# A fourth weight buffer with loads issued one chunk earlier, a descriptor area of 8 KB, and a moved product in the attention

## The chip, the cores and the metric

The kernel runs on one core of a Trainium2 chip. The metric is device time in microseconds (us) of one execution, as a median over runs.

## The reference

One layer of a streaming encoder over 512 tokens of width 2048 (chunks of 64, fp32 inputs and outputs):

```
h = rms_norm(x);  proj = h @ w_in            # 2048 x 15424, cut into 13 parts
A: o_conv = (b * conv3(c * u) * silu(conv_z)) @ w_conv_out
B: q = rms_norm(c_q) @ w_uq (16 heads, 128 + 64 rotary);  k, v = rms_norm(c_kv) @ w_ukv
   softmax(block-causal(q k^T * scale)) v, times silu(mla_z), @ w_mla_out
C: cross-attention of mem_q (4 heads of 256) into 256 memory tokens
   k, v = rms_norm(mem) @ w_mem_kv;  times silu(mem_z), @ w_mem_out
x + (sigmoid(g_conv) * o_conv + sigmoid(g_mla) * o_mla + sigmoid(g_mem) * o_mem) @ w_o
```

## The kernel before, in words

Every product is made of three matmuls (`mm3`, L161 to L163): both sides are split into a rounded high part and a low rest, and high x high, high x low and low x high are summed in PSUM. A weight chunk of 512 KB is loaded from HBM into a tile `raw`, copied to its high part `whi` by ScalarE (ACT, L154 or L277), and VectorE (DVE) subtracts to get the low part `wlo` (L155 or L278). Three of the large products (`w_h`, `w_mla_out`, `w_o`) save matmuls with sums of quarter blocks: for those DVE also forms sums of the loaded weights first (L272 to L274). TensorE then runs 42 matmuls of 256 columns a chunk.

`raw` has three buffers, `whi` and `wlo` two each. The chunks stand in one list, `queue`. `take()` is called when TensorE's program comes to a chunk: it has the split of this chunk and the next one issued, and then `begin()` issues the load of the chunk after that together with its sums, as one step. A job is a generator that yields after its load (and sums), and then after its split.

The order of the work: the memory keys and values (32 chunks of `w_mem_kv`, during which the rows of x are read for the norm (`x_rows`), `x_scale` turns their scales by four transposes, and `x_pair` builds the input tiles); the panels of `w_h` (240 loads of 512 KB, to about 1340 us); the latent attention; the memory's attention with the convolution's output product; `w_mla_out`; `w_mem_out`; `w_o`.

Each engine runs its own queue in order. The order of TensorE (PE) and of the load queue SyncE (SP) is the order in which the program issues; so is DVE's in two stretches (from the end of the memory's product to the first panels, and from `w_mem_out` to the start of `w_o`). ACT, and DVE elsewhere, get their order from the compiler's planner, which models durations. A load waits on SP until the buffer it writes is free, and whatever SP was given later waits behind it.

In the attention one turn of the loop computes the keys' and values' projection of a pair of heads (`w`, 16 units), then the queries' one. Into these units an order written by hand slots the older pair: capital letters are its first (`A`) and second (`B`) head, small letters (`a`, `b`) the next pair's. A head's steps are transposes of keys and queries, four score steps, four transposes of the probabilities, and the product with the values, which also loads the gate tile `z` for the pair (L1004) and multiplies by it on DVE (L1010). In ORDER_KV of before, `A` alone is that last product of the first head, after the fourth `w`; the second head's product is the `B` in ORDER_Q after `a a a`.

Of the kernel before, what the change touches and what calls it, by code (L numbers as in the profile page):

```python
# [20 lines left out]
F32 = mybir.dt.float32  # L21
F32R = mybir.dt.float32r
I32 = mybir.dt.int32
AF = mybir.ActivationFunctionType
ALU = mybir.AluOpType
# [5 lines left out]
P = 128  # L31
# [17 lines left out]

ORDER_KV = "2w B B B w B w A 6w B w B B B 5w"
ORDER_Q = "a a a B a a a 4w a w b b 5w a 4w a w a a w"
ORDER_KV1 = "16w"
ORDER_Q1 = "6w a a w a 2w a a a w a w b b 3w a w a w a a"
# [52 lines left out]
def body(ctx, tc, a, out):  # L108
    nc = tc.nc
    act, vec, pool = nc.scalar, nc.vector, nc.gpsimd  # L110
# [7 lines left out]
    wpool = ctx.enter_context(tc.tile_pool(name="wts", bufs=2))  # L118
# [17 lines left out]

    def raw_tile():

        return wpool.tile([P, 8, 256], F32, tag="raw", name="raw", bufs=3)

    def weight_parts():
        return (wpool.tile([P, 7, 256], F32R, tag="whi", name="whi"),
# [2 lines left out]
    def flat(t):  # L145
        return t.rearrange("p s n -> p (s n)")
# [20 lines left out]
    queue = []  # L167
# [1 line left out]
    fills = []  # L169

    def upcoming(*jobs):
        queue.extend([job, None] for job in jobs)

    def begin(at):

        if at < len(queue) and queue[at][1] is None:
            queue[at][1] = queue[at][0]()
            queue[at].append(next(queue[at][1]))

    def take(ahead=1):  # L180
        for at, entry in enumerate(queue[:1 + ahead]):
            begin(at)
            if entry[2] is None:
                entry[2] = next(entry[1])
        begin(1 + ahead)
        if fills:
            fills.pop(0)()
        return queue.pop(0)[2]

    def plain_jobs(srcs, n, cut=False, parts=(), beside=None):  # L190

        held = []
        each = 2048 // (KC * n)

        def job(at):
            def go():
                if at % each == 0:
                    t = flat(raw_tile())  # L200
                    held.append(t)
                    for c in range(min(each, len(srcs) - at)):
                        step = n if cut and at + c == 0 else KC * n
                        for o in range(0, KC * n, step):
                            nc.sync.dma_start(t[:, c * KC * n + o:c * KC * n + o + step],
                                              srcs[at + c][:, o:o + step])
                        if beside is not None:
                            beside(at + c)
                yield
                o = at % each * KC * n  # L210
                yield weights(held[at // each][:, o:o + KC * n], n, cut and at == 0,
                              parts[at % len(parts)] if parts else None)
            return go
        return [job(at) for at in range(len(srcs))]
# [52 lines left out]
    def pair_weights(src):  # L267


        f = raw_tile()  # L270
        nc.sync.dma_start(flat(f[:, 0:4]), src)
        vec.tensor_tensor(out=f[:, 4:6], in0=f[:, 1:3], in1=f[:, 0:1].to_broadcast([P, 2, 256]), op=ALU.add)  # L272
        vec.tensor_tensor(out=f[:, 6], in0=f[:, 5], in1=f[:, 1], op=ALU.add)  # L273
        vec.tensor_tensor(out=f[:, 7], in0=f[:, 6], in1=f[:, 3], op=ALU.add)  # L274
        yield
        hi, lo = weight_parts()
        act.activation(hi, f[:, 1:8], AF.Copy)  # L277
        vec.tensor_tensor(out=lo, in0=f[:, 1:8], in1=r32(hi), op=ALU.subtract)  # L278
        yield hi, lo
# [150 lines left out]
    def memory_load(c):  # L430
        if c < 8:
            mraw[c] = pst.tile([P, KC, M], F32, tag="msq", name="mraw", bufs=5)
            nc.sync.dma_start(mraw[c], a["memT"][:, c * KC:(c + 1) * KC])
# [85 lines left out]
    def staged_parts():  # L519
# [1 line left out]

    memory_load(0)
    upcoming(*plain_jobs([a["w_mem_kv"][grp][c] for grp in range(4) for c in range(8)], 512, True,
                         (staged_parts, None, None), lambda c: memory_load(c + 1)))
    work = panels(xp, a["w_h"], len(SEQUENCE), lambda n: make(n), lambda n, e: finish(n, e), "aux")
    queue.insert(32 + 15, [lambda: rotary_weights(), None])
    parts_of_x = all_parts()
    manual_dve = ExitStack()
    for grp in range(4):
        banks = [bank("acc") for _ in range(2)]  # L530

        for n in dense_units(banks, 512, mT, "T", nk=KB, before=memory_chunk if grp == 0 else None,
# [5 lines left out]
                manual_dve.enter_context(tc.manual_schedule(engines={DVE}))  # L538
            if grp == 0:
                memory_squares(c)  # L540
            if c == 2:
                while later:
                    later.pop(0)("aux")
# [30 lines left out]
                nc.scalar.dma_start(mvdram[2 * (grp - 2) + i], t)  # L574
    for _ in parts_of_x:
        pass
    begin(2)
    close_st()
    close_mt()
    pxb, close_xb = open_pool("xb", "right")  # L580
# [7 lines left out]
    def rotary_weights():  # L588
        f = flat(raw_tile())
        nc.sync.dma_start(f[:, :1024], a["w_kr"])  # L590
        vec.tensor_tensor(out=f[:, 1024:1536], in0=f[:, 0:512], in1=f[:, 512:1024], op=ALU.add)
        yield
        hi, lo = (flat(t)[:, :1536] for t in weight_parts())
        act.activation(hi, f[:, :1536], AF.Copy)
        vec.tensor_tensor(out=lo, in0=f[:, :1536], in1=r32(hi), op=ALU.subtract)
        yield hi, lo
# [525 lines left out]
    def mem_attend(head):  # L1122
# [12 lines left out]
        for i2 in range(2):  # L1135
# [16 lines left out]
            ri = pq.tile([P, 2], F32, tag="ri", name="ri", bufs=2)  # L1152
            vec.reciprocal(ri, sm)
            for ii in range(2):
                vec.tensor_scalar(out=p[:, ii], in0=p[:, ii], scalar1=ri[:, ii:ii + 1], scalar2=None,
                                  op0=ALU.mult)
                pr.append(p[:, ii])
            yield
        pts = []
# [272 lines left out]

# [10 lines left out]
```

## Time and profile before

| | |
|---|---|
| median of 3 runs | 2172.43 us (2167.9 to 2177.55) |
| the profiled execution | 2174.51 us |
| its span, first to last instruction | 2172.7 us |
| granted TensorE clock, mean over the span | 0.995 |
| busy | PE 98%, PEld (weight load) 94%, DVE 80%, ACT 46%, POOL 6% |

1.8 us of the profiled execution lie outside its span. A busy share is a sum over stages that have different limits; the clock is a share of full speed (1.0 is the upper of its two levels, 0.5 the lower one), and PE's busy time includes time at the lower level.

### The profile page before, as it was taken

What the parts mean: (1) busy time and instruction counts of PE and PEld (TensorE: products, weight loads), DVE (VectorE), ACT (ScalarE), POOL (GpSimd) and SP (SyncE); (2) the same over time, 40 slices, a digit from 0 to 9 for tenths busy, and PEclk for the clock granted to TensorE, in tenths of its full rate; (3) what the DMA queues carried; (4) which work ended last, traced back from release to release, by engine and by line L of the source; (5) the groups of instructions that cost most, each with busy time, mean ns of one, the idle gap of its engine ahead of it and who ended that gap; (6) DMA issues with size and microseconds to landing.
All of it is one profiled execution on the core that took longest, in us unless ns stands there. A gap on an engine that the chain in (4) does not pass through costs nothing.

```text
span 2172.7 us, 38855 instructions
## 1 busy us (share of the span) xinstructions
PE 2131.1 (98%) x16040; PEld 2042.4 (94%) x16040; DVE 1735.1 (80%) x2756; ACT 1003.7 (46%) x1219; POOL 135.5 (6%) x189
## 2 busy tenths in 40 slices
PE   9989999999999999999999999999999999999899
PEld 8789999999999999999999999888888789987899
DVE  5986878888888888889878885888877788757887
ACT  6743444444344344444444444777775433323333
POOL 0000000000000000000000000222211100011000
PEclk9999999999999999999999999999999999999999
DMA  8633443333333334344444436131347956667443
GB/s 324 241 105 131 152 137 127 127 127 127 127 127 127 127 127 135 119 137 132 137 131 144 135 132 243 59 122 70 119 168 265 363 165 204 203 200 213 138 149 117
DMA packets 93442, 338.52 MB, mean 156 GB/s; under 512 B 10896, under 2 KB 11152, under 8 KB 91216
## 3 DMA queue, kind: packets, MB, share of 16 engines
q1 hardware_dynamic: 70848, 252.58, 34.1%
q0 software_dynamic: 13920, 59.51, 8.6%
q10 hardware_dynamic: 8496, 23.94, 3.1%
q8 instruction: 125, 2.05, 0.4%
q14 instruction: 53, 0.43, 0.1%
HBM read 273.34 MB, written 62.65 MB: 155 GB/s over the span
## 4 chain that ended last, share of the span: by engine, by line
PE 78%; DVE 6%; DMA 4%; ACT 3%; issue 3%; POOL 0%; SPq 0%; DVEq 0%; ACTq 0%; POOLq 0%
PE acc L161 13%; PE acc L162 13%; PE acc L163 13%; PE aux L163 12%; PE aux L162 12%; PE aux L161 11%; DVE wlo L278 3%; DMA xm<-aadram 1%; PE aux L988 1%; DMA mgdram<-gt 1%; DMA raw<-in_w_h 1%; ACT whi L277 1%; DVE raw L272 1%; DMA sb<-gdram 1%; PE aux L971 1%
## 5 line engine op out<-in xcount | busy, mean ns | idle before, releaser
L277 ACT ACTIVATE whi<-raw 128x1792 fp32r<-128x1792 f32 x304 | 517.8, 1703 | 805.7 <-PE acc L162 346.2
L278 DVE TENSOR_TENSOR wlo<-raw,whi 128x1792 fp32r<-128x1792 f32 x304 | 614.4, 2021 | 200.3 <-ACT whi L277 199.7
L163 PE MATMUL aux<-xp,wlo 128*128 128x256 f32 (+1 forms) x1712 | 480.0, 280 | 5.6 <-DVE wlo L278 5.5
L162 PE MATMUL aux<-xp,whi 128*128 128x256 f32 (+1 forms) x1712 | 479.8, 280 | 0.0
L161 PE MATMUL aux<-xp,whi 128*128 128x256 f32 (+1 forms) x1712 | 479.6, 280 | 0.0
L163 PE MATMUL acc<-xp,wlo 128*128 128x256 f32 x1680 | 469.6, 280 | 2.8 <-DVE wlo L278 2.8
L162 PE MATMUL acc<-xp,whi 128*128 128x256 f32 x1680 | 469.6, 280 | 0.0
L161 PE MATMUL acc<-xp,whi 128*128 128x256 f32 x1680 | 469.4, 279 | 0.0
L163 PEld LDWEIGHTS aux<-xp,wlo 128*128 128x128 f32 (+1 forms) x1712 | 320.4, 187 | 6.7 <-DVE wlo L278 6.6
L161 PEld LDWEIGHTS aux<-xp,whi 128*128 128x128 f32 (+1 forms) x1712 | 321.0, 187 | 0.0
L162 PEld LDWEIGHTS aux<-xp,whi 128*128 128x128 f32 (+1 forms) x1712 | 321.0, 187 | 0.0
L163 PEld LDWEIGHTS acc<-xp,wlo 128*128 128x128 f32 x1680 | 314.8, 187 | 3.6 <-DVE wlo L278 3.6
L161 PEld LDWEIGHTS acc<-xp,whi 128*128 128x128 f32 x1680 | 315.3, 188 | 0.0
L162 PEld LDWEIGHTS acc<-xp,whi 128*128 128x128 f32 x1680 | 315.3, 188 | 0.0
L272 DVE TENSOR_TENSOR raw<-raw 128x512 f32<-128x512 f32 x304 | 208.0, 684 | 47.3 <-DMA raw<-in_w_h 30.2
L155 DVE TENSOR_TENSOR wlo<-raw,whi 128x1024 fp32r<-128x1024 f32 (+2 forms) x89 | 100.6, 1130 | 73.1 <-ACT whi L154 73.1
L154 ACT ACTIVATE whi<-raw 128x1024 fp32r<-128x1024 f32 (+2 forms) x89 | 87.6, 985 | 108.9 <-PE acc L162 46.0
L274 DVE TENSOR_TENSOR raw<-raw 128x256 f32<-128x256 f32 x304 | 127.9, 421 | 6.6
L273 DVE TENSOR_TENSOR raw<-raw 128x256 f32<-128x256 f32 x304 | 127.7, 420 | 5.9
L352 POOL TENSOR_TENSOR rs_r<-rs_t,mhalf 128x2 f32<-128x2 f32 (+2 forms) x71 | 69.6, 990 | 269.7 <-DVE rs_t L351 212.8
L161 PE MATMUL acc<-whi,blk 128*128 128x384 f32 (+1 forms) x224 | 84.8, 379 | 0.0
L163 PE MATMUL acc<-whi,blk 128*128 128x384 f32 (+1 forms) x224 | 80.9, 361 | 0.0
(360 smaller groups left out, 3905.0 us busy)
## 6 DMA issues: line engine op xcount, KB each, us to landing
raw<-in_w_h SPq DMA_DIRECT2D x240, 512.0 KB, 3.5
raw<-in_w_mla_out SPq DMA_DIRECT2D x32, 512.0 KB, 4.1
raw<-in_w_o SPq DMA_DIRECT2D x32, 512.0 KB, 3.6
raw<-in_w_mem_kv SPq DMA_DIRECT2D x31, 512.0 KB, 7.3
gdram<-e ACTq DMA_DIRECT2D x22, 512.0 KB, 2.8
raw<-in_w_ukv SPq DMA_DIRECT2D x16, 512.0 KB, 5.5
raw<-in_w_conv_out SPq DMA_DIRECT2D x16, 512.0 KB, 9.9
aadram<-z POOLq DMA_DIRECT2D x8, 896.0 KB, 4.0
```

What stands on the lines that cost most here:

```text
L154: act.activation(hi[:, cols], raw[:, cols], AF.Copy)
L155: vec.tensor_tensor(out=lo[:, cols], in0=raw[:, cols], in1=r32(hi[:, cols]), op=ALU.subtract)
L161: nc.tensor.matmul(o, lhsT=s[0], rhs=m[0], start=start, stop=False, skip_group_check=shared)
L162: nc.tensor.matmul(o, lhsT=s[0], rhs=m[1], start=False, stop=False, skip_group_check=shared)
L163: nc.tensor.matmul(o, lhsT=s[1], rhs=m[0], start=False, stop=stop, skip_group_check=shared)
L272: vec.tensor_tensor(out=f[:, 4:6], in0=f[:, 1:3], in1=f[:, 0:1].to_broadcast([P, 2, 256]), op=ALU.add)
L273: vec.tensor_tensor(out=f[:, 6], in0=f[:, 5], in1=f[:, 1], op=ALU.add)
L274: vec.tensor_tensor(out=f[:, 7], in0=f[:, 6], in1=f[:, 3], op=ALU.add)
L277: act.activation(hi, f[:, 1:8], AF.Copy)
L278: vec.tensor_tensor(out=lo, in0=f[:, 1:8], in1=r32(hi), op=ALU.subtract)
L352: pool.tensor_tensor(out=r, in0=t, in1=mhalf[:, :n], op=ALU.pow)
L971: nc.tensor.matmul(sb[:, :n], lhsT=qr[:, cols], rhs=krh[:, :n], start=False, stop=False)
```

## The change

The `raw` tile gets a fourth buffer. A job now yields after its load, after its sums and after its split, and `take` runs the list in three stages: this chunk and the next are split, the one after that is summed, and the one after that is loaded. A load thus stands one chunk earlier in SP's order; sums and splits keep their places. The loads of the memory's last three chunks move to SP's order behind the weights of chunks 1 to 3. The scale of the memory attention's probabilities (16 instructions of 128x256) moves from DVE to ACT. The first head's product (`A`, with its gate load) goes from the middle of ORDER_KV to its end. The area in SBUF for descriptors of DMAs that POOL issues is set to 8192 bytes.

```diff
-ORDER_KV = "2w B B B w B w A 6w B w B B B 5w"
+ORDER_KV = "2w B B B w B 9w B w B B B 3w A"
-        return wpool.tile([P, 8, 256], F32, tag="raw", name="raw", bufs=3)
+        return wpool.tile([P, 8, 256], F32, tag="raw", name="raw", bufs=4)
     def upcoming(*jobs):
-        queue.extend([job, None] for job in jobs)
-    def begin(at):
-        if at < len(queue) and queue[at][1] is None:
-            queue[at][1] = queue[at][0]()
-            queue[at].append(next(queue[at][1]))
+        queue.extend([job] for job in jobs)
+    def begin(at, stage):
+        if at < len(queue):
+            entry = queue[at]
+            if len(entry) == 1:
+                entry.append(entry[0]())
+            while len(entry) < 2 + stage:
+                entry.append(next(entry[1]))
     def take(ahead=1):
-        for at, entry in enumerate(queue[:1 + ahead]):
-            begin(at)
-            if entry[2] is None:
-                entry[2] = next(entry[1])
-        begin(1 + ahead)
+        for at in range(1 + ahead):
+            begin(at, 3)
+        begin(1 + ahead, 2)
+        begin(2 + ahead, 1)
...
         nc.sync.dma_start(flat(f[:, 0:4]), src)
+        yield
         vec.tensor_tensor(out=f[:, 4:6], in0=f[:, 1:3], in1=f[:, 0:1].to_broadcast([P, 2, 256]), op=ALU.add)
...
-                         (staged_parts, None, None), lambda c: memory_load(c + 1)))
+                         (staged_parts, None, None),
+                         lambda c: memory_load(c + 1) if c < 4 else None))
...
             if grp == 0:
                 memory_squares(c)
+                if c in (1, 2, 3):
+                    memory_load(c + 4)
...
-    begin(2)
+    begin(2, 2)
...
-                vec.tensor_scalar(out=p[:, ii], in0=p[:, ii], scalar1=ri[:, ii:ii + 1], scalar2=None,
-                                  op0=ALU.mult)
+                act.activation(p[:, ii], p[:, ii], AF.Copy, scale=ri[:, ii:ii + 1])
...
-    nc = bacc.Bacc("TRN2", target_bir_lowering=False, num_devices=1)
+    nc = bacc.Bacc("TRN2", target_bir_lowering=False, num_devices=1, dynamic_dma_scratch_size=8192)
```

## Rows read from the trace of the kernel before

**Rows 1.** The page: busy time with its share of the span, and PE and the DMA engines in 40 slices of the span (a digit is tenths).

```profile
PE 2131.1 (98%) x16040; PEld 2042.4 (94%) x16040; DVE 1735.1 (80%) x2756; ACT 1003.7 (46%) x1219; POOL 135.5 (6%) x189
...
PE   9989999999999999999999999999999999999899
...
DMA  8633443333333334344444436131347956667443
```

**Rows 2.** The waits of TensorE over the whole span: what it waited for, us in total, times, longest.

```profile
PE acc L163 <- DVE wlo L278: 13.8, 13, 2.0
PE aux L163 <- DVE wlo L278: 10.4, 10, 2.2
PE aux L359 <- DVE p L1155: 2.7, 2, 2.2
PE aux L971 <- DVE qr L958: 2.5, 8, 0.3
```

**Rows 3.** Busy time by stretch: stretch and its length; PE, PEld, DVE, ACT, POOL busy us with their instructions; granted clock; busy share of the DMA engines; GB/s.

```profile
108.00:139.00 31.00, 27.18 (x221) 26.16 (x221) 29.28 (x34) 14.81 (x12) 0.00 (x0) 1.00 0.34 107
139.00:156.00 17.00, 13.43 (x111) 13.03 (x111) 12.06 (x17) 5.37 (x4) 0.00 (x0) 1.00 0.28 95
...
165.00:180.00 15.00, 14.02 (x97) 13.93 (x97) 9.27 (x18) 4.82 (x5) 0.54 (x1) 0.77 0.54 193
...
1749.00:1760.00 11.00, 7.66 (x64) 7.26 (x63) 6.60 (x8) 3.95 (x3) 0.54 (x1) 1.00 0.67 235
...
2000.00:2049.00 49.00, 44.67 (x364) 43.00 (x364) 43.37 (x57) 17.53 (x13) 1.08 (x2) 1.00 0.44 136
2049.00:2073.00 24.00, 18.89 (x158) 18.29 (x157) 17.88 (x26) 8.74 (x6) 0.00 (x0) 1.00 0.43 152
2070.00:2080.00 10.00, 7.86 (x53) 7.66 (x53) 7.89 (x11) 2.50 (x2) 0.00 (x0) 0.83 0.51 159
```

**Rows 4.** The waits of DVE for a weight load, in the stretches 139 to 156, 1749 to 1760 and 2049 to 2073 us (in this order).

```profile
DVE raw L272 <- DMA raw<-in_w_h: 4.8, 3, 2.8
...
DVE raw L272 <- DMA raw<-in_w_mla_out: 4.6, 2, 3.4
...
DVE raw L272 <- DMA raw<-in_w_o: 6.1, 4, 2.9
```

**Rows 5.** The first of these waits in order of time (start, duration, engine, line; in brackets the idle time before it and what ended it): the low part of one chunk, the load that SP issues when it ends, and the sums that wait for this load.

```profile
135.58 2.02 DVE L278 TENSOR_TENSOR wlo<-raw,whi 128x1792 fp32r<-128x1792 f32 x1
...
137.63 0.33 SPq L271 DMA_DIRECT2D raw<-in_w_h  x1
...
141.96 0.69 DVE L272 TENSOR_TENSOR raw<-raw 128x512 f32<-128x512 f32 x1 [2.84 <-DMA raw<-in_w_h]
```

**Rows 6.** The waits of SP in 1960 to 2080 us: the load of a residual tile waits for the store of an earlier one.

```profile
SPq L1333 <- DMA out<-xr: 10.5, 1, 10.5
```

**Rows 7.** The stretch in which the inputs of `w_mla_out` are read back (columns as in rows 3), and the longest piece of the chain that ended last in it (start, us, what).

```profile
1700.00:1737.00 37.00, 37.00 (x165) 30.64 (x164) 25.48 (x21) 19.33 (x14) 3.55 (x7) 1.00 1.00 407
...
1712.12 20.79 DMA xm<-aadram
```

**Rows 8.** One turn of the attention in order of time (DVE, then PE, then ACT); the last line is the stretch of the turns that hold the moved product (columns as in rows 3).

```profile
1439.69 0.96 DVE L155 TENSOR_TENSOR wlo<-raw,whi 128x768 fp32r<-128x768 f32 x1
...
1442.00 0.68 DVE L958 TENSOR_TENSOR qr<-aux,qr 64x512 fp32r<-64x512 f32 x1
1442.71 0.69 DVE L1010 TENSOR_TENSOR z<-aux,z 128x512 f32<-128x512 f32 x1
...
1438.34 0.60 PE L359 MATMUL aux<-ident,kn 128*128 128x128 f32 x4
...
1439.57 0.47 PE L161 MATMUL aux<-pth,vh 128*128 128x512 f32 x1
...
1442.74 0.39 PE L971 MATMUL aux<-krh,qr 128*128 128x256 f32 x1 [0.33 <-DVE qr L958]
...
1462.17 0.40 PE L161 MATMUL aux<-pth,vh 128*128 128x512 f32 x1
...
1464.09 0.39 PE L161 MATMUL acc<-whi,blk 128*128 128x512 f32 x1
...
1468.21 0.60 PE L988 MATMUL aux<-ident,s 128*128 128x128 f32 x4
...
1464.36 1.45 ACT L981 ACTIVATE s<-s,ri 128x384 f32<-128x384 f32 x2
...
1390.00:1635.00 245.00, 242.33 (x1384) 215.01 (x1383) 204.39 (x591) 180.65 (x438) 54.51 (x66) 1.00 0.32 118
```

**Rows 9.** The memory's attention: the longer wait of rows 2 for the scaled probabilities in order of time, and what a scale of 128x256 took on DVE (1640 to 1720 us) and on ACT (the latent attention): count, busy us, mean ns.

```profile
1686.62 1.83 PE L359 MATMUL aux<-ident,p 128*128 128x128 f32 x8 [2.16 <-DVE p L1155]
...
L1155 DVE TENSOR_SCALAR p<-p,ri 128x256 f32<-128x256 f32 x16 | 4.8, 350 | 0.1
...
L981 ACT ACTIVATE s<-s,ri 128x256 f32<-128x256 f32 x16 | 7.9, 495 | 0.2 <-DVE ri L980 0.2
```

**Rows 10.** The start: the stretch in which x is read (columns as in rows 3), DVE's copy of its scales, and the transposes of it on PE (count, ns min/median/max, first and last start).

```profile
25.00:57.00 32.00, 32.00 (x163) 26.92 (x162) 17.90 (x26) 24.17 (x36) 3.68 (x4) 1.00 0.97 375
...
50.56 0.43 DVE L478 COPY xrows<-rs_r 128x512 f32<-128x512 f32 x1 [1.12 <-POOL rs_r L352]
...
L359 PE MATMUL aux<-ident,xrows x4: 270/272/272, 52.5 to 52.8; 128*128 128x128 f32 x4
```

More of the change, by code (lines that the diff above doesn't have):

```diff
@@ L171, in upcoming @@
     def upcoming(*jobs):
-        queue.extend([job, None] for job in jobs)
-    def begin(at):
-        if at < len(queue) and queue[at][1] is None:
-            queue[at][1] = queue[at][0]()
-            queue[at].append(next(queue[at][1]))
-    def take(ahead=1):
-        for at, entry in enumerate(queue[:1 + ahead]):
-            begin(at)
-            if entry[2] is None:
-                entry[2] = next(entry[1])
-        begin(1 + ahead)
+        queue.extend([job] for job in jobs)
[6 more added lines that the diff above has]
+                entry.append(next(entry[1]))
+    def take(ahead=1):
+        for at in range(1 + ahead):
+            begin(at, 3)
+        begin(1 + ahead, 2)
+        begin(2 + ahead, 1)
         if fills:
             fills.pop(0)()
-        return queue.pop(0)[2]
+        return queue.pop(0)[4]
     def plain_jobs(srcs, n, cut=False, parts=(), beside=None):
@@ L271, in pair_weights @@
         nc.sync.dma_start(flat(f[:, 0:4]), src)
+        yield
         vec.tensor_tensor(out=f[:, 4:6], in0=f[:, 1:3], in1=f[:, 0:1].to_broadcast([P, 2, 256]), op=ALU.add)
@@ L523, in body @@
     upcoming(*plain_jobs([a["w_mem_kv"][grp][c] for grp in range(4) for c in range(8)], 512, True,
-                         (staged_parts, None, None), lambda c: memory_load(c + 1)))
+                         (staged_parts, None, None),
+                         lambda c: memory_load(c + 1) if c < 4 else None))
     work = panels(xp, a["w_h"], len(SEQUENCE), lambda n: make(n), lambda n, e: finish(n, e), "aux")
-    queue.insert(32 + 15, [lambda: rotary_weights(), None])
+    queue.insert(32 + 15, [lambda: rotary_weights()])
     parts_of_x = all_parts()
@@ L590, in rotary_weights @@
         nc.sync.dma_start(f[:, :1024], a["w_kr"])
+        yield
         vec.tensor_tensor(out=f[:, 1024:1536], in0=f[:, 0:512], in1=f[:, 512:1024], op=ALU.add)
```

## The prediction, made before the changed kernel ran

> **What bounds the kernel now.** I read the page first. TensorE is busy 98% of the span, and its slices show it full from the second tenth to past the half [rows 1]. So the kernel is bound by TensorE's program, and a change can give back only what TensorE idles, 2172.7 - 2131.1 = 41.6 us, and what it loses at the lower clock. Next I read its list of waits: 24.2 us in 23 waits for a low weight part (L278), 2.7 us for scaled probabilities, and eight waits of 0.3 us for the rotary queries [rows 2]. Then the table by stretch, to see where these waits lie and whether DVE, which makes the low parts, was full there. In 108 to 139 and 2000 to 2049 us TensorE idled 3.8 and 4.3 us and DVE was busy 94% and 89%: DVE's own work was late. In three other stretches DVE had idle time: TensorE idled 17.00 - 13.43 = 3.57 us in 139 to 156, 11.00 - 7.66 = 3.34 in 1749 to 1760, and 24.00 - 18.89 = 5.11 in 2049 to 2073 [rows 3]. There DVE's list of waits names the weight loads, with 4.8, 4.6 and 6.1 us [rows 4]. The timeline shows how: a low part that began at 135.58 ended, SP issued a load at 137.63 into the buffer that this freed, and the sums, which stand in DVE's queue ahead of other work, waited for it until 141.96 [rows 5]. With three buffers a load begins only when a buffer falls free, and DVE stands at its sums before it has landed. In the last stretch SP had also stood 10.5 us behind a residual tile's load, with weight loads queued after it [rows 6].
>
> **The fourth buffer.** It takes away no instruction on PE; DVE's sums and low parts keep their lengths. A load may now be issued when the low part one chunk further back ends. A chunk takes TensorE about 5 us (240 chunks of `w_h` in some 1230 us), and the load of rows 5 took 141.96 - 137.63 = 4.3 us, so it lands before its sums come up [rows 5]. DVE's waits of 15.5 us [rows 4] then go, and since in each stretch they are longer than TensorE's idle time, I count all of it: 3.57 + 3.34 + 5.11 = 12.0 us. Bounds: 12.0 at most; nothing, if DVE's freed time is used up by work that is late anyway, as in the two DVE-full stretches, where I count no gain. Behind the last of the gaps the granted clock is 0.83 over 10 us [rows 3], part of it at the lower level: 0.17 x 10 = 1.7 us of work, counted as won with its gap. In 165 to 180 us it is 0.77, 0.23 x 15 = 3.4 us, beside 1.0 us of idling [rows 3]. This follows a wait for ACT, not for a load, so I count nothing, and keep 4.4 us for the low end.
>
> Every other load on SP now stands behind one more weight load. In 200 to 1340 us nothing can be lost by it, since TensorE is full there. It can be lost where the DMA engines are full. Around 1700 to 1737 us they are busy 1.00 at 407 GB/s, and the chain runs through the read-back of a `w_mla_out` input for 20.79 us [rows 7]. One more weight load of 512 KB (524,288 bytes) ahead of it costs 1.3 us at that rate. If transfers shared the bandwidth evenly, the input would lose only part of that; if two loads stand ahead it loses 2.6. I take 1.3, bounds 0 and 2.6. The Trainium skill (DMA: Bandwidth & Descriptors, Queues, rings and completion order) says that each DMA engine consumes the descriptors of a ring in order, which speaks against pulling loads ahead of anything more urgent: by it the whole 512 KB counts for each load ahead, and with two the sum below would be 1.3 us worse. The 20.79 us for one input, in a stretch of full engines, agree with queueing.
>
> **The start.** The rows of x feed a DVE copy that ends at 50.99 us, and the transposes on PE come at 52.5 [rows 10], so 1.5 us of delay are free. The third and fourth row tiles can now have 1 MB of weights (two chunks) more in front of them, 2.8 us at 375 GB/s with the DMA engines 0.97 busy [rows 10]. But the third row tile waits for a free row buffer in any case (two buffers for four tiles), while the weights drain. I take 0; bounds are 0 and 2 x 2.8 - 1.5 = 4.1 us lost. The three memory loads moved behind weights belong to chunks 5 to 7, several chunks ahead of need; nothing.
>
> **The moved product.** It takes 1464.09 - 1462.17 = 1.92 us on PE [rows 8] wherever it stands, in seven turns (six of the loop, one under the convolution). Where it stood it covered the first part of the softmax of the second head: PE reached the transposes at 1468.21, and the last scale on ACT ended at 1465.81, 2.4 us earlier [rows 8]. Two more units (nine for seven) replace the product; a unit is 3 x 512 columns and the product 3 x 1408, so two take 2 x 1.92 x 512 / 1408 = 1.4 us by its rate, and PE comes there about 0.5 us sooner. The slack of 2.4 hides that. At its new place it puts 1.92 us of PE work ahead of the transposes of the next pair. The wait of 0.33 us at L971 for the rotary queries comes about because DVE first makes a low weight part (to 1440.65) and then the low parts of keys and queries [rows 8]. With 1.92 us more, less the 0.69 us of the gate multiply that moves along, DVE is ahead and the wait goes: 7 x 0.33 = 2.3 us. Bounds: all idling of that stretch, 245.00 - 242.33 = 2.7 us [rows 8], and a loss that is a rival below. The gate's load moves with the product on SP; behind one more weight load, at a DMA share of 0.32 [rows 8]: nothing.
>
> **The scale on ACT.** Sixteen scales of 350 ns leave DVE; the same shape took ACT 495 ns [rows 9]. The wait of 2.16 us before the transposes at 1686.62 [rows 9] came from DVE's queue, but the last exponentials on ACT came just before, and the four copies are longer there. I take 0; bounds are a loss of 16 x 0.145 = 2.3 us and the 2.7 us of the wait.
>
> **The descriptor area.** No wait of a POOL transfer in the trace names anything but its data. I count 0. The Trainium skill (SBUF — State Buffer, the size table) gives 16 KiB as the usual reserve for descriptors; 8 KB would be half of it, and no row shows what a full one costs.
>
> **Sum.** 12.0 + 1.7 - 1.3 + 2.3 = 14.7 us off the profiled execution of 2174.5 us gives 2159.8. That execution lies 2.1 us above the median of 2172.4 (runs from 2167.9 to 2177.6), so by the median it is 2157.7, and I say 2158. A change of 0.5% (10.9 us) is about what a measurement of this kernel can tell from none.
>
> **Rivals.**
> (1) *DVE stays the limit.* Once the loads are there, the low parts still wait for ACT, and ACT for PE's release of `whi`; half of the gaps come back as waits for the same line. For it: 108 to 139 and 2000 to 2049 us, with the loads in time and 8.1 us of gaps. Against it: DVE's waits for loads exceed the gaps in all three stretches. It gives half of 13.7, less 1.3, plus 2.3: 7.9 us, 2164.5.
> (2) *The rows of x are late.* The start loses up to 4.1 us: about 2162. For it: DMA share 0.97 and 1.5 us of slack. Against it: SP's wait for the row buffers.
> (3) *The gate multiply is late; slower than before.* PSUM has four `aux` banks: the first head's product, then the transposes of keys, queries and rotary queries, then the second head's product, which takes the first one's bank and must wait for its multiply on DVE. The transposes take 1439.57 - 1438.34 = 1.23 us, so this multiply must end 1.23 us after the first product. If the planner puts it behind the rotary low part, which ended 1442.68 - 1439.57 = 3.11 us after the transposes, the second product waits 3.11 + 0.69 = 3.8 us, in seven turns 26.6 us: 2172.4 - 12.4 + 26.6 = 2186.6. It decides from 12.4 / 7 = 1.8 us of lateness on. For it: DVE's order here is the planner's, and the second head's multiply, at 1442.71, stood right behind the rotary low part [rows 8]. Against it: the moved multiply becomes ready 1.23 us before the last of the low parts' inputs.
> (4) *The loads were no limit.* SP stays behind other waits (rows 6 is one) and the loads come no earlier: 2172.
>
> **Chances and range.** Forecast 0.50; (1) 0.22; (2) 0.10; (3) 0.13; (4) 0.05. Faster by over 0.5% (below 2161.6): the forecast and 0.04 of (2), 0.54. Within 0.5%: (1), the rest of (2), (4) and a mild (3) of 0.02, 0.35. Slower: 0.11. The low end adds 4.4 us (165 to 180), 2.7 (scale), 1.3 (no lateness of the read-back) and 0.4 (attention) to the sum: 2149, and I put 2147. The high end takes in (1), (2), (4) and the median's own scatter: 2176. The forecast's own range is 2149 to 2165.
>
> **What will show it.** Right: in the three stretches no wait of DVE for `raw`, and TensorE's total for L278 near 12 instead of 24 us; SP's loads issued a low part earlier; a clock near 1.0 around 2075 us; no wait at L971 in the middle turns; L988 without waits. Wrong: the wait for L278 unchanged with DVE idle no more (1); a wait of PE at the scale transposes near 52 us (2); a wait of the second head's product for L1010 (3); unchanged issue times (4).

## The result, and the profile after

The changed kernel takes 2163.1 us, median of 8 runs (2160.3 to 2165.8), against 2174.6 for the kernel before, median of 8 runs beside it: a ratio of 0.9948, 95% interval 0.9936 to 0.9959, so 11.4 us. A second measurement (below) gave 0.9952 (0.9935 to 0.9969). The forecast was 14.7 us off, 2158 us. The profiled execution's span is 2160.7 us, 12.0 less than before's. This line answers to [rows 1]:

```profile
PE 2122.6 (98%) x16040; PEld 2037.7 (94%) x16040; DVE 1728.2 (80%) x2740; ACT 1010.8 (47%) x1235; POOL 130.9 (6%) x189
```

TensorE (PE) is busy 8.5 us less with the same instructions, and idles 38.1 in place of 41.6 us. So most of the 12 us of these two executions lies in PE's busy time, not in its gaps. The waits of PE in the changed kernel (as [rows 2]; L282 is the low part that was L278, L276 the sums that were L272):

```profile
PE acc L163 <- DVE wlo L282: 13.6, 12, 2.6
PE aux L163 <- DVE wlo L282: 8.2, 10, 3.0
PE aux L977 <- DVE z L1019: 2.5, 6, 0.4
PE aux L363 <- ACT p L1164: 2.4, 3, 1.7
...
PE aux L363 <- DVE xrows L482: 0.7, 1, 0.7
```

The waits for low parts fell from 24.2 to 21.8 us, not to the 12 that I named as the sign of success. Nor does this total tell the kernels apart: a second profile of the changed kernel has 18.9 us, and the kernel with the descriptor area alone, which keeps the buffers and loads of before, 19.7. The rotary queries' wait is gone from the lines above, and a wait of the same total stands there, for a gate multiply on DVE.

The waits of DVE for weight loads over the whole span say more. Before, and then in the changed kernel:

```profile
DVE raw L272 <- DMA raw<-in_w_h: 30.2, 24, 3.9
DVE raw L272 <- DMA raw<-in_w_mla_out: 8.6, 8, 3.4
DVE raw L272 <- DMA raw<-in_w_o: 8.1, 6, 2.9
```

```profile
DVE raw L276 <- DMA raw<-in_w_h: 31.8, 22, 3.6
DVE raw L276 <- DMA raw<-in_w_o: 2.4, 5, 0.6
DVE raw L276 <- DMA raw<-in_w_mla_out: 2.1, 5, 0.6
```

In `w_mla_out` and `w_o` most of them went; in `w_h` nothing changed. The stretches of [rows 3] in the changed kernel, the later ones moved by what had been gained by then:

```profile
139.00:156.00 17.00, 12.54 (x105) 12.14 (x105) 11.88 (x17) 5.37 (x4) 0.00 (x0) 1.00 0.26 90
165.00:180.00 15.00, 14.06 (x109) 13.98 (x108) 9.03 (x17) 5.57 (x5) 0.54 (x1) 0.89 0.57 211
1745.30:1756.30 11.00, 9.71 (x80) 9.29 (x79) 9.63 (x15) 3.41 (x2) 2.15 (x4) 1.00 0.87 311
1991.40:2040.40 49.00, 41.70 (x337) 40.08 (x338) 42.92 (x57) 17.35 (x12) 1.08 (x2) 1.00 0.41 125
2040.40:2064.40 24.00, 22.07 (x186) 21.87 (x187) 20.62 (x31) 8.89 (x6) 0.00 (x0) 1.00 0.53 189
2061.40:2071.40 10.00, 10.00 (x88) 10.00 (x87) 8.53 (x12) 3.41 (x2) 0.00 (x0) 1.00 0.47 159
```

The first gap grew, from 3.57 to 17.00 - 12.54 = 4.46 us. In `w_mla_out` 3.34 became 1.29. In the 73 us of `w_o` (fourth and fifth line) 9.44 became 9.23: the later gap shrank from 5.11 to 1.93, the earlier one grew from 4.33 to 7.30.

A stage's length, from the first or last matmul on a tile that only this stage reads to the next such matmul, needs no count of idling. In us, one profile of each kernel; the experiments are told below:

| | to 1st panel | `w_h` | attention | memory's attention | `w_mla_out` | `w_mem_out` | `w_o` |
|---|---|---|---|---|---|---|---|
| before | 107.5 | 1230.1 | 313.1 | 88.5 | 163.8 | 89.7 | 180.0 |
| changed | 106.7 | 1228.9 | 310.9 | 89.0 | 160.0 | 88.6 | 176.6 |
| changed, second profile | 108.5 | 1227.7 | 311.0 | 88.7 | 160.0 | 87.4 | 176.6 |
| buffer, loads and area only | 108.7 | 1231.2 | 313.0 | 86.0 | 160.5 | 87.4 | 176.7 |
| moved product only | 107.5 | 1230.0 | 310.8 | 88.5 | 163.7 | 89.8 | 178.4 |
| changed, three buffers | 107.6 | 1229.9 | 311.0 | 88.7 | 163.3 | 88.2 | 174.8 |
| changed, scale on DVE | 106.2 | 1231.3 | 310.9 | 86.0 | 160.4 | 87.7 | 176.8 |
| changed, sums two back | 108.9 | 1232.4 | 318.5 | 88.7 | 158.8 | 87.4 | 174.3 |
| changed, adds on POOL | 107.5 | 1232.1 | 310.9 | 88.7 | 160.5 | 87.3 | 182.0 |
| changed, product a unit earlier | 107.2 | 1230.8 | 312.8 | 88.8 | 161.3 | 88.4 | 175.8 |
| changed, short adds | 108.6 | 1231.1 | 311.0 | 89.1 | 159.3 | 88.2 | 177.3 |
| combined | 106.4 | 1224.9 | 311.0 | 86.0 | 158.8 | 87.4 | 174.3 |
| area only | 107.5 | 1228.3 | 314.4 | 86.1 | 162.5 | 89.1 | 178.2 |

### The profile page after: what moved, and what is told of

Its sections match the earlier page's. It is cut to its first block, busy times and chain, and to the rows that moved or that the text cites. A ratio compares the mean times of both kernels' runs of the same rounds, so it can differ in the third digit from the quotient of the medians.

```text
span 2160.7 us, 38707 instructions
## 1 busy us (share of the span) xinstructions
PE 2122.6 (98%) x16040; PEld 2037.7 (94%) x16040; DVE 1728.2 (80%) x2740; ACT 1010.8 (47%) x1235; POOL 130.9 (6%) x189
## 4 chain that ended last, share of the span: by engine, by line
PE 84%; DVE 5%; ACT 2%; DMA 2%; issue 1%; POOL 0%; DVEq 0%; ACTq 0%; POOLq 0%
PE acc L161 14%; PE acc L163 14%; PE acc L162 14%; PE aux L161 13%; PE aux L163 13%; PE aux L162 13%; DVE wlo L282 2%; PE aux L363 1%; PE aux L997 1%; DMA raw<-in_w_h 1%; ACT whi L281 1%; DVE raw L276 0%; PE aux L977 0%; PE aux L980 0%; PE aux L978 0%
## 5 line engine op out<-in xcount | busy, mean ns | idle before, releaser
L282 DVE TENSOR_TENSOR wlo<-raw,whi 128x1792 fp32r<-128x1792 f32 x304 | 614.8, 2022 | 204.2 <-ACT whi L281 203.5
L276 DVE TENSOR_TENSOR raw<-raw 128x512 f32<-128x512 f32 x304 | 208.3, 685 | 36.5 <-DMA raw<-in_w_h 31.8
L154 ACT ACTIVATE whi<-raw 128x1024 fp32r<-128x1024 f32 (+2 forms) x89 | 87.7, 986 | 101.4 <-PE acc L162 43.3
L278 DVE TENSOR_TENSOR raw<-raw 128x256 f32<-128x256 f32 x304 | 127.9, 422 | 6.3
L356 POOL TENSOR_TENSOR rs_r<-rs_t,mhalf 128x2 f32<-128x2 f32 (+2 forms) x71 | 65.2, 929 | 276.7 <-DVE rs_t L355 217.2
```

Of the source, the lines that this page charges most:

```text
L154: act.activation(hi[:, cols], raw[:, cols], AF.Copy)
L356: pool.tensor_tensor(out=r, in0=t, in1=mhalf[:, :n], op=ALU.pow)
```

## The experiments

**The parts apart.** First the buffer, the staged loads, the moved memory loads and the area, without the moved product and with the scale on DVE:

```diff
-ORDER_KV = "2w B B B w B 9w B w B B B 3w A"
+ORDER_KV = "2w B B B w B w A 6w B w B B B 5w"
-                act.activation(p[:, ii], p[:, ii], AF.Copy, scale=ri[:, ii:ii + 1])
+                vec.tensor_scalar(out=p[:, ii], in0=p[:, ii], scalar1=ri[:, ii:ii + 1], ...)
```

> The changed kernel without its moved product and with the scale of the memory attention back on DVE: what is left is the fourth weight buffer with its staged loads, the moved memory loads and the 8 KB area. Between the two traces the attention's stretch came out 2.2 us shorter and the stages around it 9.8 us. If the parts add, this kernel keeps about 9.5 us of the 11.4 and stands near 2165, ratio to before 0.9955. By the rival that the loads were no limit (the gain is the move's and scatter's), it stands within 2 us of before. The rotary wait of 0.33 us should be back in the attention's turns either way.

Measured: 0.9968 (0.9957 to 0.9979), 2164.7 us, about 7 us off where 9.5 were expected. The attention stands at its old 313.0 with the rotary wait back, and the stages behind it are short. Second, the kernel before with the new ORDER_KV alone:

> The kernel before with only the first head's product moved to the end of the keys' and values' product. My sum gave it 7 x 0.33 = 2.3 us; the trace of after shows the old wait gone, and a new one of 0.42 us in six turns before the third score block, with the stage 2.2 us shorter. If the stage's gain is the move's: about 2 us faster, ratio near 0.999, the new wait present with three buffers too. If the gain of the stage came from the fourth buffer: no change, at most 0.5 us either way.

Measured: 0.9987 (0.9971 to 1.0002), as a total not told apart from no change. The attention is 310.8, and the rest is nearly as before: the stage's 2.1 to 2.3 us are the move's, and no other part of the change gives them.

**What took the place of the rotary wait.** A turn of the attention in the changed kernel (DVE, then PE; the first and the last PE line are the first matmul of the score step and the first one behind it), and then the same two matmuls before:

```profile
1438.89 0.68 DVE L967 TENSOR_TENSOR qr<-aux,qr 64x512 fp32r<-64x512 f32 x1
1439.61 0.88 DVE L134 SCALAR_TENSOR_TENSOR vl<-acc,kr__97,vh 128x256 fp32r<-128x256 f32 x2
1440.40 0.68 DVE L1019 TENSOR_TENSOR z<-aux,z 128x512 f32<-128x512 f32 x1
...
1439.21 0.28 PE L977 MATMUL aux<-kTh,qTh 128*128 128x256 f32 x1
...
1439.85 0.28 PE L981 MATMUL aux<-krl,qr 128*128 128x256 f32 x1
...
1441.13 0.44 PE L977 MATMUL aux<-kTh,qTh 128*128 128x384 f32 x1 [0.42 <-DVE z L1019]
...
1442.12 0.34 PE L161 MATMUL acc<-whi,blk 128*128 128x384 f32 x1
```

```profile
1441.58 0.28 PE L968 MATMUL aux<-kTh,qTh 128*128 128x256 f32 x1
...
1444.57 0.44 PE L161 MATMUL acc<-whi,blk 128*128 128x384 f32 x1
```

The rotary low part is now in time. But DVE does two low parts of values, which PE does not wait for here, ahead of the second head's gate multiply, and the third score block takes the PSUM bank that this multiply frees: 0.42 us in six turns. This is rival (3) in a mild form, one bank further on. So the wait was exchanged, not removed, and a listed wait is not what it costs: such three score blocks take 2.07 us where nothing waits (at 1457.57 us before), 1444.57 - 1441.58 = 2.99 us with the old wait of 0.33 and 1442.12 - 1439.21 = 2.91 us with the new one of 0.42, because matmuls beside a wait stand longer, too. The net of 2.1 us is made up otherwise. The six turns of the loop are each 0.18 us shorter (the score step begins every 35.11 us before, every 34.93 now), which is 1.1 us, and the turn under the convolution has neither wait (2.95 us before, 2.10 now), which is 0.85. A trial of the product one unit earlier (`2w A w` in place of `3w A`):

> The changed kernel with the moved product one unit earlier: the keys' and values' product ends 2w A w in place of 3w A. The unit (3 x 512 columns, 0.7 us on PE) then stands between the first head's product and the transposes of keys and queries, and gives DVE 0.7 us to get to the second head's gate multiply. If the new wait of 0.42 us is a matter of this lateness, it goes in all six turns, the attention's stage falls from 310.9 to about 308.4, and the old wait for the rotary queries does not return; 2.5 us faster than the changed kernel. If DVE's order follows along, the wait stays and the time too.

Measured: 0.9957 (0.9942 to 0.9972), near 2166 us, and PE's list shows the old wait in full:

```profile
PE aux L980 <- DVE qr L967: 2.5, 8, 0.3
```

The new wait is gone, the old one is back, the stage is 312.8. Neither expectation held in full. I read it as one lateness of DVE, and the place of the product decides at which of the two PE meets it; no run takes that lateness itself away.

**Buffer or order.** The changed kernel with `bufs=3` for `raw`:

> The changed kernel with three buffers of the weight tile in place of four; the loads still stand one chunk earlier in the order of SP. Theory (the buffer lets the load start): with three a load still begins only when the low part two chunks back ends, the DVE waits for loads of w_mla_out (1.9 us in after) and w_o come back to about 6 each, the gap of 1749 to 1760 us comes back, and the kernel is 4 to 9 us slower than the changed one, near 2170. Rival (the place in the order is what counts, not the buffer): within 2 us of the changed kernel, 2163.

Measured: 0.9979 (0.9968 to 0.9991), 2166.7 us, between the two; by the ratios about 6 us slower than the changed kernel, as the theory had it. The two stages answer differently. 28 us from just before the first matmul of `w_mla_out`, first before, then with three buffers, then the changed kernel:

```profile
1736.00:1764.00 28.00, 23.01 (x178) 21.82 (x178) 21.69 (x26) 8.74 (x6) 3.25 (x6) 1.00 0.54 181
```

```profile
1736.00:1764.00 28.00, 23.45 (x192) 22.81 (x191) 21.88 (x29) 10.69 (x7) 3.26 (x6) 1.00 0.55 193
```

```profile
1733.00:1761.00 28.00, 26.70 (x213) 25.83 (x212) 25.37 (x32) 10.53 (x7) 3.25 (x6) 1.00 0.60 217
```

PE idles 5.0, 4.6 and 1.3 us: here the buffer is what helps. (One profile with three buffers, that of the area-only kernel, idles 2.6 us there, so a part of the difference is scatter.) In `w_o` the kernel with three buffers is the shortest of the three (174.8), and DVE's waits for the loads of `w_o`, 8.1 us before, are 1.3 us with three buffers and 2.4 in the changed kernel; so there the gain is that of the earlier place in SP's queue, as far as one profile with three buffers shows it. SP's wait of [rows 6], ahead of which a weight load now stands, was 4.6 us with three buffers and still 12.1 us in the changed kernel.

**The order of the sums.** Why did the gap of 139 to 156 us grow? The changed kernel's DVE, in order:

```profile
137.44 0.68 DVE L276 TENSOR_TENSOR raw<-raw 128x512 f32<-128x512 f32 x1
...
142.47 0.69 DVE L276 TENSOR_TENSOR raw<-raw 128x512 f32<-128x512 f32 x1 [3.01 <-DMA raw<-in_w_h]
143.20 0.42 DVE L277 TENSOR_TENSOR raw<-raw 128x256 f32<-128x256 f32 x1
143.54 2.02 DVE L282 TENSOR_TENSOR wlo<-raw,whi 128x1792 fp32r<-128x1792 f32 x1
```

As in [rows 5], sums wait for a load, and the low part behind them, whose high part ACT had finished at 141.33, starts only at 143.54. With a fourth buffer there is one more chunk whose sums the planner can put ahead: they are those of a later chunk, but they stand there. Counting from the start of `w_h` shows it. Ahead of the seventh low part, the late one in both kernels (143.03 us before, 143.54 now), SP had issued nine loads before and ten in the changed kernel; and DVE had begun the sums of eight chunks before and of nine now. The load came one chunk earlier, and so did the sums that wait for it. First test, on the kernel before: the sums may follow only the low part of the chunk ahead of them.

```diff
+        with tc.issue_after(lows[0].ins):          # the last low part
             vec.tensor_tensor(out=f[:, 4:6], ...)  # the three sums
+        lows[:] = [vec.tensor_tensor(out=lo, ...)]
```

> The kernel before (three buffers) with one thing added: the three sums of a chunk may enter DVE's queue only after the low part of the chunk before it. No instruction is added. Theory (the stall is one of order: the planner puts sums whose load has not landed ahead of a low part that TensorE is about to need): DVE's waits at the sums no longer delay the low part; TensorE's idle time in 139 to 156 us falls from 3.57 to under 1 us, that of 1749 to 1760 and 2049 to 2073 likewise, in all up to 12 us faster, near 2162, ratio about 0.995, as much as the fourth buffer gives. Rival (the loads themselves are late, so the low part that follows the sums is late in any order): the gaps stay, ratio 1.00; it may be slower if the planner's order was needed elsewhere.

Measured: 1.0944 (1.0924 to 1.0964), 205 us slower. DVE's waits for loads are gone from its list, but PE waits 162.7 us for low parts (here L166 and L282), and `w_h` alone takes 1402 us in place of 1230. In the middle of `w_h` (DVE, then ACT):

```profile
602.03 2.02 DVE L282 TENSOR_TENSOR wlo<-raw,whi 128x1792 fp32r<-128x1792 f32 x1 [1.82 <-ACT whi L281]
603.97 0.69 DVE L276 TENSOR_TENSOR raw<-raw 128x512 f32<-128x512 f32 x1
...
605.15 0.43 DVE L278 TENSOR_TENSOR raw<-raw 128x256 f32<-128x256 f32 x1
607.40 2.02 DVE L282 TENSOR_TENSOR wlo<-raw,whi 128x1792 fp32r<-128x1792 f32 x1 [1.82 <-ACT whi L281]
...
605.66 1.70 ACT L281 ACTIVATE whi<-raw 128x1792 fp32r<-128x1792 f32 x1 [3.67 <-DVE raw L278]
```

Held so close, low part, sums and ACT's copy form one chain: 607.40 - 602.03 = 5.37 us a chunk, where the kernel before begins a low part every 4.95 (615.40 to 620.35) and PE is full. Sums must run one chunk further ahead of the low parts. So the second test, on the changed kernel, holds them to the low part two chunks back (`lows[-2]`):

> The changed kernel, with an edge that lets the three sums of a chunk into DVE's queue only after the low part of the chunk two before it (the earlier experiment held them to one before and lost 200 us). Theory (with the fourth buffer the planner takes sums whose load has not landed ahead of an urgent low part): in 139 to 156 us the low part of 143.5 starts near 141.4, TensorE idles 2 us less there (4.46 to about 2.4), DVE's waits for loads of w_h fall below 20 us, and the kernel gains 1 to 3 us. Rival (steady state needs sums earlier than that): TensorE waits for low parts all along w_h and the kernel is slower by tens of us. Third: the order was like this already, no change.

Measured: 0.9977 (0.9966 to 0.9988), slower than the changed kernel; yet in the places of the theory it did what the theory says. No wait of DVE for a load of `w_h`, `w_mla_out` or `w_o` is left in its list. In 139 to 156 us, taken 2.2 us later because its first panel comes that much later, PE idles 1.2 us in place of 4.5, and `w_mla_out` and `w_o` are the shortest of the table (158.8, 174.3). The loss is elsewhere: the attention's stage is 7.6 us longer, where PE waits 4.4 us for a load of the latents (`latdram`) and the clock falls to 0.83 in the 20 us behind it, and `w_h` has a gap of 2.8 us near 1030 us with a clock below full behind it. The edge helps in the places where loads are late, and hurts in others, where I take it that the planner had used its freedom well.

**The scale.** The changed kernel with its sixteen scales on DVE again:

> The changed kernel with the sixteen scales of the memory attention's probabilities back on DVE; all else as changed. From the first pulse of the memory's scores to the first of w_mla_out the profiles give 88.5 us (before), 89.0 (after, scale on ACT), 88.7 (three buffers, scale on ACT), 88.5 (move only, scale on DVE) and 86.0 (first experiment: four buffers, scale on DVE). Theory (the scale on ACT loses what an earlier w_mla_out start would give): 86.0 here too, kernel 2.5 to 3 us faster than the changed one, about 2160, the wait of 1.7 us near 1660 us gone. Rival (the 86.0 came only from a clock that did not fall in that one execution): the stage shows 88 to 89 again or the median equals the changed kernel's within 1 us.

Measured: 0.9946 (0.9931 to 0.9961), 2161.3 us against 2162.0 for the changed kernel beside it: not told apart as a total, but the stage shows it, 86.0 in place of 88.7 to 89.1. The window 1660 to 1665 us, changed kernel and then this one (columns as in [rows 3]):

```profile
1660.00:1665.00 5.00, 3.25 (x14) 2.34 (x14) 1.45 (x4) 5.00 (x16) 0.00 (x0) 0.83 0.91 357
```

```profile
1660.00:1665.00 5.00, 4.45 (x28) 3.48 (x27) 4.58 (x16) 5.00 (x15) 0.00 (x0) 1.00 1.00 347
```

ACT is full in both. In the changed kernel the scales (L1164) stand between its exponentials (L1159), DVE is nearly empty (1.45), and PE waits for a scale (ACT, then PE):

```profile
1661.27 0.91 ACT L1164 ACTIVATE p<-p,ri 128x256 f32<-128x256 f32 x2
1662.06 0.56 ACT L1159 ACTIVATE p<-aux,nm,mqs 128x256 f32<-128x256 f32 x1
...
1661.83 1.17 PE L363 MATMUL aux<-ident,p 128*128 128x128 f32 x6 [1.68 <-ACT p L1164]
```

The stage of the kernel before, 88.5, holds a clock of 0.76 and 0.90 behind its gap; the area-only kernel, with the same code, shows 86.1 without one. With the scale on ACT the stage takes 88.7 us also in the three profiles whose clock is 1.00 over it (the second one of the changed kernel, sums two back, adds on POOL), so the clock is not the reason. So the scale on ACT costs 2.7 us against an execution with the clock up, and little against the one that I had.

**The clock.** The changed kernel once more:

> The changed kernel unchanged, profiled a second time and timed beside the others. If the stretches of lower clock are tied to the program, they stand at the same places as in the first profile (170, 1660, 2155 us) and not at 228, 1988 or 2070. If they vary from execution to execution, they stand elsewhere, with TensorE's idle times by stage unchanged within 0.3 us; then the 1.7 us that the forecast counted for one dip, and the 6.6 us by which the two first profiles differ in clock, are no property of the change. Time: ratio to before 0.994 to 0.996.

Measured: 0.9952 (0.9935 to 0.9969). Fifty microseconds of `w_o` from 25 us after its first matmul, first profile and second:

```profile
2009.10:2059.10 50.00, 42.84 (x351) 41.62 (x352) 43.39 (x63) 17.84 (x13) 0.00 (x0) 1.00 0.40 137
```

```profile
2008.30:2058.30 50.00, 44.32 (x351) 43.10 (x352) 43.37 (x63) 17.85 (x13) 0.00 (x0) 0.97 0.40 137
```

The same 351 matmuls of the same program; the granted clock was 1.00 in one execution and 0.97 in the other, where one slice of 5 us near 2040 us stood at 0.66. PE was busy 1.5 us longer and idle 1.5 us less, so its idle time did not stay within the 0.3 us that I expected, and the stage took 176.6 us both times. Here PE waits for DVE anyway, and the lower clock only fills its waits. Of the places with a clock below full, 165 to 180 us shows one in every profile; those near 1660 and 2155 us of the changed kernel's first profile are gone in its second; that of the kernel before at the start of `w_o` (near 1990 us) is missing in the first profile of the changed kernel and there in the second, and those near 228 and 2070 us return in neither, nor in the area-only and the moved-product-only kernels, which have the buffers and loads of before.

**DVE's own work in `w_o`.** Two tests that take the residual adds off DVE. On POOL (`nc.gpsimd` for `vec`):

> The changed kernel with the fourteen residual adds of w_o (128x512, 0.69 us each on DVE) on POOL instead. Theory (in 2000 to 2049 us DVE's own work is the limit, 43.8 of 49 us busy): four adds of 0.69 us leave the stretch from 2034 to 2043, the low part there comes up to 2.6 us earlier, TensorE's idle time in 2000 to 2049 falls from 7.64 to about 5, and the kernel gains 1 to 2.6 us. Rival (the loads are what is late there, the sums wait for them): idle stays 7 to 8, no gain. Loss: POOL is slow and the store and the buffer come later, so the next residual load on SP holds up weight loads; then waits of SP for a store over 10 us and some us slower.

Measured: 0.9988 (0.9975 to 1.0001); `w_o` takes 182.0 us. DVE, then POOL:

```profile
2033.61 2.98 DVE L282 TENSOR_TENSOR wlo<-raw,whi 128x1792 fp32r<-128x1792 f32 x1
2036.51 1.77 DVE L276 TENSOR_TENSOR raw<-raw 128x512 f32<-128x512 f32 x1
...
2033.45 1.26 POOL L1350 TENSOR_TENSOR xr<-e,xr 128x512 f32<-128x512 f32 x1 [32.10 <-DVE e L326]
2034.67 3.05 POOL L1350 TENSOR_TENSOR xr<-e,xr 128x512 f32<-128x512 f32 x1
```

The first add of the pair takes 1.26 us on POOL, and the low part that begins within it takes 2.98 us in place of 2.02. The second add, which begins within the low part, takes 3.05 us, and the sum behind the low part 1.77 in place of 0.69: the two engines' instructions hold each other up in turn, and DVE loses 2.0 us where it was to win 1.3. The test says nothing on DVE's load, so the other one cuts the adds short (`xr[:, f, :64]`):

> The changed kernel with the fourteen residual adds of w_o cut from 512 to 64 columns (the rest of the output stays the residual): loads, stores and order as before, 0.6 us less on DVE per add. Theory (DVE's own work is the limit in 2000 to 2049 us): TensorE's idle time there falls from 7.6 to about 5 or below and w_o takes 174 to 175 us in place of 176.6. Rival (the weight load is late there, and the sums stand before an urgent low part): idle stays above 7, DVE waits longer at the sums instead.

Measured: 0.9960 (0.9945 to 0.9974), `w_o` 177.3 us: no gain. The stretch shows something of both:

```profile
2044.05 0.35 DVE L1350 TENSOR_TENSOR xr<-e,xr 128x64 f32<-128x64 f32 x2
2046.32 0.69 DVE L276 TENSOR_TENSOR raw<-raw 128x512 f32<-128x512 f32 x1 [1.92 <-DMA raw<-in_w_o]
...
2047.39 2.02 DVE L282 TENSOR_TENSOR wlo<-raw,whi 128x1792 fp32r<-128x1792 f32 x1
```

PE's idle time in the 49 us from 15.9 us after the stage's first matmul falls from 7.6 to 5.0 us (6.4 in the second profile of the changed kernel, with a clock of 0.97 as here), and the low part of 2047.39 begins 60.1 us into the stage in place of 61.2: that is the theory's sign. But a part of the time that the adds gave back became a wait at the sums of a late load, longer (1.92 us) than those of 0.53 and 0.57 in the changed kernel at this place; over the stage DVE's waits for loads grew from 2.4 to 10.4 us, and the next 26 us hold 1.7 us of idling where the changed kernel had none. Less work on DVE alone thus did not shorten the stage; the order edge, which takes no work off DVE, did (174.3).

**The area.** The kernel before with `dynamic_dma_scratch_size=8192` alone:

> The kernel before with only the descriptor area of POOL's transfers set to 8192 bytes. My sum gave it nothing: ratio between 0.9985 and 1.0015, stage times those of before within 0.5 us (1230.1 for w_h, 313.1 for the attention, 163.8 for w_mla_out). If transfers that POOL issues had waited for room for descriptors, or do so with less room, the stages that read the gates back (w_mla_out 163.8, w_mem_out 89.7) would change by more than 1 us. Since the program is else that of before, its profile also shows whether the stretches of lower clock of before (228, 1682, 1988 and 2070 us) recur at their places: if they do not, they are no property of the kernel.

Measured: 0.9988 (0.9977 to 0.9999). The interval leaves out 1 by a hair. Its stages stand up to 2.4 us from those of before, in both directions, where I had allowed 0.5: so far do two profiles of what is nearly one program differ. Whether the area gives nothing or a little (up to 0.23%, 5 us) stays open.

**What helped, together.** The changed kernel with the scale on DVE and the two-back edge only in the first 16 chunks of `w_h`, in `w_mla_out` and in `w_o`:

```diff
+        chunk[0] += 1
+        held = chunk[0] <= 16 or chunk[0] > 240
+        with tc.issue_after(lows[-2].ins) if held else ExitStack():
```

> The changed kernel with the scale back on DVE, and the edge of two chunks back only where it shortened a stage: the first 16 chunks of w_h, w_mla_out and w_o. With the edge everywhere the profile gave 1.2 us less in w_mla_out, 2.3 less in w_o and 3.9 us less idling in 110 to 156 us, but 7.6 more where the attention begins and gaps of 2.8 us inside w_h; the scale on DVE gave 2.7 less in the memory's stage. If the parts add: 1.2 + 2.3 + 3.9 + 2.7 = 10 us less than the changed kernel, near 2152, ratio to before 0.990. If the planner moves the gaps elsewhere, as it did at 165 and 1030 us: no better than 2161.

Measured: 0.9904 (0.9887 to 0.9920), 2153.4 us: faster than both kernels, some 10 us below the changed one, as the parts had it. Its DVE at the gap of 139 us:

```profile
136.86 0.68 DVE L281 TENSOR_TENSOR raw<-raw 128x512 f32<-128x512 f32 x1
...
140.37 2.03 DVE L287 TENSOR_TENSOR wlo<-raw,whi 128x1792 fp32r<-128x1792 f32 x1 [1.90 <-ACT whi L286]
142.32 1.29 DVE L281 TENSOR_TENSOR raw<-raw 128x512 f32<-128x512 f32 x2
...
146.51 2.02 DVE L287 TENSOR_TENSOR wlo<-raw,whi 128x1792 fp32r<-128x1792 f32 x1 [1.57 <-ACT whi L286]
```

No sum waits for a load: the low part that began at 143.54 begins at 140.37, and the sums, done after it, find their data landed. In the count from above, the seventh low part now has ten loads and the sums of seven chunks ahead of it, against ten and nine in the changed kernel. PE idles 17.00 - 15.84 = 1.16 us in the stretch:

```profile
139.00:156.00 17.00, 15.84 (x132) 15.43 (x131) 13.48 (x21) 6.96 (x6) 0.00 (x0) 1.00 0.35 114
```

## Why the prediction was right in its time, and where its steps failed

The measured 2163.1 us lies in the forecast's own range, but nearer to rival (1)'s 2164.5 than to the forecast's 2158, and several terms erred in directions that offset each other.

- **The fourth buffer, 12.0 us.** The three terms came out so. 139 to 156 us: 3.57 forecast, nothing won. `w_mla_out`: 3.34 forecast; 160.0 us in both profiles (159.3 to 161.3 in the others with four buffers and no order edge) in place of 162.5 to 163.8 in the four profiles with three buffers, so 2.5 to 3.8 won, and by the buffer, as said. `w_o`: 5.11 forecast; 176.6 us against 180.0, 178.4 and 178.2 in three profiles without the staged loads, so 1.6 to 3.4 won, and by the order of the loads rather than by the buffer. The step that failed is "it lands before its sums come up": I held the sums in place and moved the loads. The sums' place on DVE is the planner's, and in the first gap it moved along with the buffer: nine chunks' sums ahead of the seventh low part in place of eight, and a wait of 3.01 us at them. With the order edge there the gap closes to 1.16 us. Rival (1) had the size of it, half of the gaps coming back, but not the cause: not DVE's work, its order.
- **The clock, 1.7 us.** Failed as a term. The lower clock near 2075 us did vanish in the profile of the changed kernel, but the second profile shows that such a stretch can come and go in the same program, and cost nothing where PE waits for DVE; and the one near 2070 us is missing, too, in two profiles with the buffers and loads of before.
- **The read-back, 1.3 us lost.** Not seen. With the scale on DVE the memory's stage, which ends with this input, takes 86.0 us with four buffers and 86.1 with three and the loads of before. The step that failed is that this input's delay is PE's: in 1690 to 1745 us PE's list names no wait at all, before or after, and ACT, which reads the input, waited 4.4 us for it before and 0.6 after. By the rule that the prediction takes from the Trainium skill (DMA: Bandwidth & Descriptors, Queues, rings and completion order) the loss would be 1.3 us or twice that; no run here shows either, and since PE does not wait for this input, it does not put the rule to the test.
- **The moved product, 2.3 us.** 2.1 to 2.3, on the point, but by luck. The step "the wait goes" held in the turn under the convolution alone; in the six others rival (3)'s wait took its place, and the list of waits shows 2.5 us before and 2.5 after. And the price was too low: a listed wait of 0.33 us cost the score step 2.99 - 2.07 = 0.92 us. The 2.1 us are 0.85 in that one turn and 0.18 in each of the six others; that they meet 7 x 0.33 is chance.
- **The scale, nothing.** 2.7 us lost at the same clock, just past the bound of 2.3. I had seen that ACT's exponentials came just before the wait and did not ask what else was queued on ACT: the scales delay later exponentials, too.
- **The start, nothing.** The 0.7 us wait at the transposes of x is there (rival 2), and the first panel comes at 106.2 to 108.9 us, against 107.5: nothing that can be told. The four profiles with a panel at 108.5 or later are those with a granted clock of 0.72 to 0.94 between 10 and 20 us.
- **Not forecast:** `w_mem_out`, 89.7, 89.8 and 89.1 us without the staged loads and 87.3 to 88.6 with them, some 1.5 us. The stage's length goes with DVE's waits in it for the input `mg`: 3.3, 3.0 and 2.4 us without the staged loads, 0 to 1.9 with them, 1.9 and none in the two profiles of one program. So a part of it is scatter; what moved this input, no run shows.

From the two profiles of the changed kernel against those without the parts in question, the stages add up to 2.1 + 3.3 + 1.5 + 2.3 won and 1.2 lost in the memory's stage (88.85 against a mean of 87.7 of before, moved product only and area only), with 1.2 of `w_h`: 9.2 us. The 1.2 of `w_h` are not shown to be the change's, since the five other profiles with four buffers and no edge show 1230.8 to 1232.1 there. The two ratios say 10.4 and 11.3; the remaining 1 to 2 us is less than the same program's profiles differ by (spans of 2172.7 and 2166.1 us for before and area only).

## What to carry to other kernels

A deeper buffer helps where the engine that consumes it comes to its queue's next item with the data landed: where an in-order queue is filled by a planner, look at which item stands ahead of the urgent one before counting a load's wait as won, and let a buffer and an order edge go together. Such an edge is worth setting only in the stretches whose trace shows the stall; everywhere it cost 200 us at one distance and several at another. A wait in a list is not its price: compare the stretch around it with one that does not wait. Judge a part by the length of its stage over several profiles, since idle time and clock trade places from one execution to the next.

## What the runs showed of the hardware

While POOL ran elementwise adds of two tensors in SBUF, DVE's instructions with two inputs in SBUF took about 1 us longer each (2.02 to 2.98, 0.69 to 1.77), and an add of 1.26 us took 3.05 when it began within such an instruction. The Trainium skill (SBUF — State Buffer, SBUF: two separate sides) says that the two engines lock a shared port pair for a whole instruction in just this case, and that the one that comes second is blocked until the first is done. The trace agrees: the low part ends 1.88 us after the first add, the second add 1.14 us after the low part, and the sum 0.55 us after the second add, each 0.12 to 0.14 us less than it takes alone (2.02, 1.26, 0.69). And the granted clock in one place of one program was 1.00 in one execution and 0.66 in the next, with the stage's length unchanged at 176.6 us.
